# Moving the two-operand work of two stages from GpSimd to VectorE in a two-layer hybrid trunk

## The chip, the cores and the metric

The kernel runs on one core of one Trainium2 chip. The metric is the device time of one execution in microseconds, from the first to the last instruction of the program; three executions of the kernel before gave 3420.28, 3424.99 and 3428.63 us, median 3424.99. Four engines matter here: TensorE (PE in the rows) for products of matrices, VectorE (DVE), ScalarE (ACT) and GpSimd (POOL). SyncE (SP) issues the transfers between DRAM and the on-chip memory SBUF. The matmuls' sums land in PSUM.

## The reference

Two layers run over 1024 latent tokens and 256 context tokens, with 1024 channels. Every layer has an input projection whose columns go to three groups of heads, their joint output projection, and a feed-forward part with a gated convolution. The last layer needs no result for the context.

```
h = rms_norm(x, norm1) * (1 + scale) + shift
c_q, c_kv, k_rope, u, q_s, k_s, v_s = split(h @ w_in)
ya = latent_attention(c_q, c_kv, k_rope)      # 6 heads, all keys; q and k normed, with rotary angles
yb = s5_bidirectional(u)                      # 16 groups of 16 channels, 64 complex states, 2 directions
yc = windowed_attention(q_s, k_s, v_s)        # 6 heads over 2 key heads, a window of 128, sinks
x = x + gate * (concat(ya, yb, yc) @ w_out)
x = x + gate2 * conv_ffn(rms_norm(x, norm2) * (1 + scale2) + shift2)

s5:  a_bar = exp(lam * dt);  b_bar = (a_bar - 1) / lam * b
     h[t] = a_bar * h[t-1] + b_bar u[t];  y[t] = Re(c h[t]) + d u[t];  then a gelu and a gate
rms_norm(x, g) = x * rsqrt(mean(x * x) + eps) * g
```

## The kernel before, in words

All large products are made of three matmuls over a high and a low part of each operand (`ah`, `al`, `wh`, `wl`). The program is one sequence of stages per layer. A list scheduler orders the instructions of each engine by priority and by readiness, so neighbouring pieces of the program are interleaved on each engine; an engine then executes its own list strictly in order.

- **Input projection** (0 to 275 us in layer 0, 1850 to 2085 us in layer 1). For pairs of token tiles (128 tokens each), `s1_pair` makes the windowed keys, `s3` keys and values of the latent attention, `s5q` its queries, `s7` the windowed queries. Each squares its product on ScalarE, sums on VectorE (`ssq`), takes a reciprocal root (`rinv`, by `rsqrt`: two integer steps and three Newton steps, eleven VectorE instructions), multiplies by it (`mulr`), rotates by the angle tables (`rope`, on GpSimd) and stores to DRAM (`kd`, `vd`, `qd`, `sqd`).
- **U projection** (275 to 309 us, 2085 to 2120 us): the S5 channels `u`, in six tiles of the program's tile `f`, stored to `ud`. Loads of the first head's keys (`kn`), queries (`qn`) and values follow on the same SP queue.
- **Latent attention** (309 to 724 us, 2120 to 2492 us): 132 and 120 steps over heads and chunks of queries. It makes scores twice: once for the row maxima (`b<-kh,qh`, read by VectorE as `mx`), and once for the exponentials (`s`), and then the sums over values (`av`). A generator `s5()` runs as `side` between these steps, to a share of its own steps, so that it is done after 5/6 of them (`S5N` holds the number of its steps).
- **S5** works by quarters of the 16 groups. `tables(k)` makes output and input maps (`cv`, `q`) as products of powers with the matrices, `phases(k)` makes rotations `E` for 160 windows by doubling (48 instructions of growing width), both on GpSimd. `maps`, `inputs`, `outputs` are mainly transposes and matmuls on TensorE; `recur` multiplies by `E` on VectorE (`t`, `z`, then a scan over `sv`, then `u`, `Sg`). Ahead of them stand some 150 small VectorE instructions which make the parameters (`s`, `pw`) of the layer from `a_re`, `a_im` and `log_dt`; their transposes on TensorE read `pst`.
- **Modulation vectors** of later stages (`macc<-mw,srow,macc`) run on VectorE beside the attention of layer 0.
- Windowed attention, output projection and feed-forward follow (to 1850 us, and 2492 to 3426 us in layer 1).

The helpers record most operations on one line each in the kernel before: matmuls L65, transposes L74, ScalarE L77, `tt` (two tensors) L80, `ts` (scalars) L93 and L95, `stt` L98. In the order of the kernel after, all VectorE instructions stand at L50, and `tt` on GpSimd at L95.

Of the kernel before, what the change touches and what calls it, by code (L numbers as in the profile page):

```python
# [32 lines left out]
def trunk(ctx, tc, x, c, ctxt, c_ctx, w_mod, b_mod, norm1, w_in, q_lora_g, w_uq, kv_lora_g, w_ukv,  # L33
# [4 lines left out]
    V, S, G, PE = nc.vector, nc.scalar, nc.gpsimd, nc.tensor  # L38
# [19 lines left out]
    mhalf = const.tile([128, 4], F32, name="mhalf")  # L58
# [45 lines left out]
    def load_split(hi, lo, raw, srcs, scale=None):  # L104
        """DRAM pieces into raw, then hi = the rounded value and lo = what is left of it."""
# [9 lines left out]
    class Wsets:  # L115
        """Rotating sets of (rounded, rest, raw) weight tiles over the pools that are open."""
# [49 lines left out]

    def k8(t):
# [73 lines left out]
    def mod_cols(psf, pl, acc, l, nm, k0, n, nj):  # L241
        """Sums over the partitions of acc, n blocks of 128 columns for each of nj."""
# [13 lines left out]
    def mod_gen(l, nm, nj, pl, psf, w):  # L256
        """One modulation vector, with the sums over the rows on the vector engine."""
# [15 lines left out]
    def norm_stats(big, sm, psf, xs, ci, rn, o=0, n=None, eng=None):  # L273
        """rn[p, i] = 1 / rms of token i * 128 + p of the chunk (or of n of its tokens from o)."""
# [3 lines left out]
        for k in range(8):  # L278
# [18 lines left out]
    def norm_apply(tb, rbt, psf, rn, xs, at, A, sh, ci, o=0, n=None, eng=G):  # L297
# [217 lines left out]
    for l in range(2):  # L515
# [63 lines left out]
        def rope(xv, tab, g, t, nh, half, eng=None):  # L579
# [4 lines left out]
            if t >= NL:  # L584
                mul(xv, xv, g.unsqueeze(1).to_broadcast(sh), eng)
                return
# [1490 lines left out]
```

## Time and profile before

| | |
|---|---|
| time of the runs | 3420.28, 3424.99, 3428.63 us |
| span of the profiled execution | 3426.8 us; no other work around the span is in its time |
| TensorE busy | 3253.7 us, 95% |
| VectorE busy | 2339.9 us, 68% |
| ScalarE busy | 1167.5 us, 34% |
| GpSimd busy | 486.9 us, 14%, 787 instructions |

The shares are means over the whole span. How the stages differ is read from windows in time; a recorded VectorE or GpSimd instruction counts as busy from its start to its end, also when it is held up between.

### The profile page before, as it was taken

How to read it: one execution, taken by the hardware profiler on the slowest of the kernel's cores; microseconds unless marked ns; L12 is line 12 of the kernel's file. 1: busy time of each engine (PE TensorE's matmuls, PEld its weight loads, DVE VectorE, ACT ScalarE, POOL GpSimd, SP SyncE). 2: the span in 40 equal slices, each digit the busy share in tenths (PEclk: the TensorE clock that was granted, in tenths of full speed). 3: DMA queues.
4: the chain of work that ended last, by engine and by line, in shares of the span. 5: the costliest groups of instructions: out<-in, count | busy, mean ns of one | idle time of the engine just before them, and what ended most of it. 6: DMA issues, size and time to landing. Idle time of an engine off the chain costs nothing. (4 is left out here: it accounts for less than half of the span.)

```text
span 3426.8 us, 43150 instructions
## 1 busy us (share of the span) xinstructions
PE 3253.7 (95%) x15950; PEld 2597.1 (76%) x15950; DVE 2339.9 (68%) x4391; ACT 1167.5 (34%) x2076; POOL 486.9 (14%) x787
## 2 busy tenths in 40 slices
PE   8999769999999999999999999679999999999999
PEld 5897446667888888888888887446677788888888
DVE  7778786885687766667666768776762665555655
ACT  3532225555152222222223442234563422222221
POOL 2332561000020000000000432471000100000000
PEclk9999789999999999999999999789999999999999
DMA  7434111333512222222212344010324111111211
GB/s 247 132 87 125 32 50 41 98 116 100 166 47 77 64 73 73 64 65 78 62 59 68 101 117 116 18 31 23 87 71 124 44 44 49 56 43 43 62 37 56
DMA packets 401325, 260.84 MB, mean 76 GB/s; under 512 B 173647, under 2 KB 370393, under 8 KB 401113
## 3 DMA queue, kind: packets, MB, share of 16 engines
q1 hardware_dynamic: 400466, 257.80, 26.0%
q8 instruction: 126, 2.06, 0.2%
q14 instruction: 86, 0.70, 0.1%
q10 hardware_dynamic: 647, 0.26, 0.0%
HBM read 206.22 MB, written 49.46 MB: 75 GB/s over the span
## 5 line engine op out<-in xcount | busy, mean ns | idle before, releaser
L65 PE MATMUL u<-ah,wh 128*128 128x512 f32 (+1 forms) x1760 | 649.9, 370 | 2.3 <-ACT ah L77 1.6
L65 PE MATMUL u<-al,wh 128*128 128x512 f32 (+1 forms) x1760 | 648.9, 369 | 1.4 <-POOL al L80 1.1
L65 PE MATMUL u<-ah,wl 128*128 128x512 f32 (+1 forms) x1760 | 648.3, 368 | 0.0
L77 ACT ACTIVATE wh<-raw 128x1024 fp32r<-128x1024 f32 (+3 forms) x184 | 189.2, 1038 | 720.5 <-PE d L65 292.2
L98 DVE SCALAR_TENSOR_TENSOR cv<-u,par,cv 128x511 f32<-128x511 f32 (+2 forms) x616 | 326.1, 555 | 135.6 <-ACT cv L77 130.4
L65 PEld LDWEIGHTS u<-al,wh 128*128 128x128 f32 x1760 | 332.3, 189 | 58.2 <-POOL al L80 2.2
L65 PEld LDWEIGHTS u<-ah,wh 128*128 128x128 f32 x1760 | 332.0, 189 | 57.8 <-ACT ah L77 1.8
L65 PEld LDWEIGHTS u<-ah,wl 128*128 128x128 f32 x1760 | 332.2, 189 | 55.3
L80 DVE TENSOR_TENSOR wl<-raw,wh 128x1024 fp32r<-128x1024 f32 (+3 forms) x184 | 220.1, 1200 | 160.0 <-ACT wh L77 158.9
L98 DVE SCALAR_TENSOR_TENSOR x<-d,g,x 128x512 f32<-128x512 f32 (+2 forms) x307 | 209.5, 685 | 108.8 <-PE d L65 108.6
L98 DVE SCALAR_TENSOR_TENSOR macc<-mw,srow,macc 128x256 f32<-128x256 f32 (+1 forms) x364 | 231.3, 660 | 67.1 <-DMA mw<-in_w_mod_dram 65.8
L77 ACT ACTIVATE cv<-u,par,par 128x512 f32<-128x512 f32 (+1 forms) x220 | 159.7, 728 | 323.1 <-PE u L65 320.9
L65 PE MATMUL av<-p,v 128*65 128x512 f32 (+1 forms) x504 | 260.7, 601 | 0.0
L77 ACT ACTIVATE p<-s 128x512 f32<-128x512 f32 (+1 forms) x252 | 147.6, 586 | 236.4 <-PE s L65 233.1
L65 PE MATMUL d<-ah,wh 128*128 128x512 f32 (+2 forms) x614 | 224.8, 366 | 1.8 <-DVE x L98 1.6
L65 PE MATMUL d<-al,wh 128*128 128x512 f32 (+2 forms) x614 | 223.5, 364 | 0.0
L65 PE MATMUL d<-ah,wl 128*128 128x512 f32 (+2 forms) x614 | 223.4, 364 | 0.0
L1336 DVE TENSOR_REDUCE mx<-b 128x1 f32<-128x512 f32 (+1 forms) x300 | 165.6, 586 | 47.6 <-PE b L65 46.3
L65 PE MATMUL b<-kh,qh 96*128 96x512 f32 (+1 forms) x300 | 124.7, 462 | 63.0 <-DVE ql L98 46.0
L65 PE MATMUL s<-qh,kh 97*128 97x512 f32 (+1 forms) x252 | 154.0, 611 | 0.0
L65 PEld LDWEIGHTS b<-kh,qh 96*128 96x128 f32 x300 | 57.9, 199 | 114.5 <-DVE ql L98 50.8
L65 PE MATMUL av<-sp,sv 128*65 128x384 f32 x320 | 129.0, 492 | 6.5 <-ACT sden L77 3.4
(373 smaller groups left out, 6689.4 us busy)
## 6 DMA issues: line engine op xcount, KB each, us to landing
raw<-in_w_up_dram SPq DMA_DIRECT2D x88, 512.0 KB
mw<-in_w_mod_dram SPq DMA_DIRECT2D x224, 128.0 KB
raw<-in_w_down_dram SPq DMA_DIRECT2D x44, 512.0 KB
mw<-in_w_mod_dram SPq DMA_DIRECT2D x48, 256.0 KB
wm<-in_w_mod_dram SPq DMA_DIRECT2D x16, 512.0 KB
xd<-x SPq DMA_DIRECT2D x32, 256.0 KB
raw<-in_w_in_dram SPq DMA_DIRECT2D x14, 512.0 KB
sqd<-sqb SPq DMA_DIRECT2D x36, 192.0 KB
```

The costliest lines, as they stand in the source:

```text
L65: PE.matmul(out, lhsT, rhs, start=start, stop=stop)
L77: S.activation(out, in_, func, **kw)
L80: (eng or V).tensor_tensor(out, a, b, op=op)
L98: V.scalar_tensor_tensor(out, a, s, b, op0=op0, op1=op1)
L1336: V.tensor_reduce(mx[:, j, i:i + 1], ps[:, :w], axis=AX.X, op=ALU.max)
```

## The change

Everything with two tensor operands on GpSimd in the input projection, the norms and S5 is given to VectorE, apart from the roots. A reciprocal root is now one instruction on GpSimd, the power of -1/2 (`rsqrt_pool`, as the norms had it before). The multiplication by it, with its stores, is put off by one pair of token tiles (`scaling`). The parameters of S5 are made for both layers at once, 2 x 16 columns wide, beside the U projection of layer 0, and go through DRAM (`pmd`, read as `pm`); layer 1 makes none. They hold two power tables `EP` and `EQ`, of which `phases` is one complex product instead of the doubling. Six copies per quarter-independent table, `nct`, `cpx` and `cpl` go from VectorE to ScalarE. S5 yields more often, and its steps are weighed by the VectorE work that they issued (`Metered`, `Weighed`).

```
@@ helpers
+    class Metered:
+            def call(out, *args, **kw):
+                self.load += 100 + max(int(np.prod(a.shape[1:])) for a in (out, *args[:1]) if hasattr(a, "shape"))
+                return fn(out, *args, **kw)
+    V = Metered(nc.vector)
-    mhalf = const.tile([128, 4], F32, name="mhalf")
+    mhalf = const.tile([128, 12], F32, name="mhalf")
-    S5N = [161, 138]
+    S5N = [175700, 166800]
+    class Weighed(Side):
+        def to(self, k):
+            while self.k < k and not self.done:
+                at = V.load
...
+                self.k += 200 + V.load - at
-    def rsqrt(pl, dst, v, shape, tag):
-        i = pl.tile(shape, I32, tag=tag + "i", name="rsi")
-        w = pl.tile(shape, F32, tag=tag + "w", name="rsw")
-        ts(i, v.bitcast(I32), 1, op0=ALU.logical_shift_right)
-        ts(dst.bitcast(I32), i, -1, 0x5F3759DF)
-        for _ in range(3):
-            stt(w, v, -0.5, dst, ALU.mult, ALU.mult)
-            mul(w, w, dst)
-            stt(dst, w, 1.5, dst, ALU.add, ALU.mult)
@@ input projection
-                add(ss[z], ss[z], sq, (eng or (G if k < 6 else V)) if z else V)
+                add(ss[z], ss[z], sq)
-            if k % 2 and eng is G:
-                act(t, t, AF.Identity, bias=sh[:, k, j:j + 1])
-                sub(lo, t, f32(hi), G)
-            else:
-                stt(lo, t, sh[:, k, j:j + 1], f32(hi), ALU.add, ALU.subtract)
+            stt(lo, t, sh[:, k, j:j + 1], f32(hi), ALU.add, ALU.subtract)
-            mul(t1, xv, tb[:, :, :, 0:w].to_broadcast(sh), eng)
+            mul(t1, xv, tb[:, :, :, 0:w].to_broadcast(sh))
...
-            add(xv, t1, t2, eng)
+            add(xv, t1, t2)
-            r = kp.tile([128, 2 * nh], F32, tag="rinv", name="rinv", bufs=2)
-            rsqrt(kp, r, ssq, [128, 2 * nh], f"hn{nh}")
+            r = kp.tile([128, 2 * nh], F32, tag="rinv", name="rinv", bufs=3)
+            rsqrt_pool(r, ssq, 2 * nh)
+        def scaling(fn):
+            if waiting:
+                waiting.pop()()
+            if fn:
+                waiting.append(fn)
...
-            rope(qb, tab_sq, gain["sgq"], t0, 6, 32)
             ssq = ssq_of(sq, 6, 64)
             ts(ssq, ssq, 1.0 / 64, EPS)
-            mulr(qb, qb, rinv(ssq, 6), 6, 64)
-            for i in range(2):
-                for z in range(2):
-                    nc.sync.dma_start(out=sqd[:, t0 + i, :, z, :].rearrange("h p d -> p h d"), in_=qb[:, i])
+            rr = rinv(ssq, 6)
+            rope(qb, tab_sq, gain["sgq"], t0, 6, 32)
+
+            def scaled():
+                mulr(qb, qb, rr, 6, 64)
+                for i in range(2):
+                    for z in range(2):
+                        nc.sync.dma_start(out=sqd[:, t0 + i, :, z, :].rearrange("h p d -> p h d"), in_=qb[:, i])
+            scaling(scaled)
@@ S5
-                mul(t1, pr, cr, G)
-                mul(t2, pi, ci_, G)
-                sub(cv[0], t1, t2, G)
+                mul(t1, pr, cr)
+                yield
+                mul(t2, pi, ci_)
+                yield
+                sub(cv[0], t1, t2)
+                yield
...
-                V.tensor_copy(cpx, unc[:, :, cs])
-                V.tensor_copy(cpl, un[:, :, cs])
+                act(cpx, unc[:, :, cs])
+                act(cpl, un[:, :, cs])
...
-                while n < 160:
-                    m = min(n, 160 - n)
-                    s2 = [128, GQ, m]
-                    er, ei2 = (z[lev][:, gs].unsqueeze(2).to_broadcast(s2) for z in (ec, ei))
-                    cmul(E[0][:, :, n:n + m], E[1][:, :, n:n + m], E[0][:, :, 0:m], E[1][:, :, 0:m], er, ei2, s2,
-                         "pm", G)
+                a = [z[:, :, gs].rearrange("p t g -> p g t").unsqueeze(3).to_broadcast(sh) for z in EP]
+                b = [z[:, :, gs].rearrange("p t g -> p g t").unsqueeze(2).to_broadcast(sh) for z in EQ]
+                Ev = [z.rearrange("p g (a b) -> p g a b", a=10) for z in E]
+                yield from cmul(Ev[0], Ev[1], a[0], a[1], b[0], b[1], sh, "pm")
@@ U projection
+        if l == 0:
+            prm_pool, close_prm = open_pool("prm", side=sd)
+            prms = Side(s5_params(prm_pool, lambda: cps.tile([128, 512], F32, tag="b", name="b", bufs=3)), 30)
+            prms.to(1)
...
-                if f * 3 + ci == 2:
-                    side.to(6)
+                if l == 0:
+                    prms.share(f * 3 + ci + 1, 6)
```

On GpSimd, at the first quarter of S5 in layer 0, the order before holds the tables (`pm`, `cm` are products, `cv`, `q` the maps) and then the doubling of `E`, 60 instructions for a quarter; the first of them are:

```order
L80 TENSOR_TENSOR pm_3830<-pc_3808,ct_3780 128x640
L80 TENSOR_TENSOR pm_3831<-pc_3809,ct_3781 128x640
L80 TENSOR_TENSOR pm_3832<-pc_3808,nct 128x640
L80 TENSOR_TENSOR cv_3826<-pm_3830,pm_3831 128x640
L80 TENSOR_TENSOR pm_3833<-pc_3809,ct_3780 128x640
L80 TENSOR_TENSOR cm_3840<-pq_3810,bb_3776 128x512
L80 TENSOR_TENSOR cv_3827<-pm_3832,pm_3833 128x640
```

After, between the last roots of the input projection and the windowed attention, GpSimd's order has memsets alone; its first rows there are:

```order
L95 TENSOR_TENSOR rinv<-ssq,mhalf 128x12 x2
L95 TENSOR_TENSOR kvr<-kvv,mhalf 128x2
L95 TENSOR_TENSOR rinv<-ssq,mhalf 128x12 x11
L1376 MEMSET v_0_2819 128x10
L1376 MEMSET v_1_2823 128x10
L1256 MEMSET Sg_4092 64x4
```

On VectorE, where `recur` of the first quarter meets the attention's row maxima, the order before is:

```order
L1336 TENSOR_REDUCE mx<-b 128x1 x2
L80 TENSOR_TENSOR strip<-strip,b 16x4x16
L1340 TENSOR_REDUCE nm<-mx 128x4
L80 TENSOR_TENSOR t_4345<-E_4065,sv_4296 128x640
L80 TENSOR_TENSOR t_4348<-E_4066,sv_4296 128x640
L80 TENSOR_TENSOR t_4346<-E_4066,sv_4297 128x640
L80 TENSOR_TENSOR t_4347<-E_4065,sv_4297 128x640
```

After, the phases of the quarter stand ahead of it on the same engine, cut up by the attention's own work:

```order
L50 TENSOR_TENSOR cm_3944<-pm 128x640
L50 SCALAR_TENSOR_TENSOR kl<-b,gcol,kh_2825 96x256
L50 TENSOR_TENSOR cm_3945<-pm 128x640
L50 TENSOR_TENSOR cm_3946<-pm 128x640
L50 TENSOR_TENSOR strip<-strip,b 16x4x16
L50 TENSOR_TENSOR E_3942<-cm_3944,cm_3945 128x640
L50 SCALAR_TENSOR_TENSOR macc<-mw,srow,macc 128x512 x2
L50 TENSOR_TENSOR cm_3947<-pm 128x640
L50 SCALAR_TENSOR_TENSOR ql<-b,gcol,qh 96x512
L50 TENSOR_REDUCE mx<-b 128x1 x6
```

The twelve products of a quarter's tables and the six of its phases have so moved from the first list into this one.

On TensorE, in the U projection of layer 0, the transposes of `kn` stand before its last tiles (`f`) in the order before:

```order
L65 MATMUL f<-ah,wl 128x256
L74 MATMUL b<-ident,kn 96x128 x5
L65 MATMUL f<-ah,wh 128x512
L65 MATMUL f<-al,wh 128x512
L65 MATMUL f<-ah,wl 128x512
L65 MATMUL f<-ah,wh 128x512
L74 MATMUL b<-ident,kn 96x128 x5
```

After, they stand one tile of `f` later, behind the first transpose of `pst`:

```order
L80 MATMUL f<-ah,wl 128x512
L89 MATMUL b<-ident,pst_0_2858 128x16
L89 MATMUL b<-ident,kn 96x128 x4
L89 MATMUL b<-ident,pst_1_2861 128x16
L89 MATMUL b<-ident,pst_2_2864 128x16
L89 MATMUL b<-ident,kn 96x128 x4
L80 MATMUL f<-ah,wh 128x512
```

The transposes of `pst`, which came some 45 rows behind the first `kn` before, are now mixed with them.

## Rows read from the trace of the kernel before

**Rows 1.** The page: engines' totals, and two lines of the 40 slices.
```profile
PE 3253.7 (95%) x15950; PEld 2597.1 (76%) x15950; DVE 2339.9 (68%) x4391; ACT 1167.5 (34%) x2076; POOL 486.9 (14%) x787
...
POOL 2332561000020000000000432471000100000000
PEclk9999789999999999999999999789999999999999
```

**Rows 2.** Windows by stage: each engine's busy us (instructions), granted clock, DMA share, GB/s.
```profile
309.00:330.00 21.00, 21.00 (x86) 12.91 (x85) 20.99 (x151) 9.74 (x19) 0.00 (x0) 1.00 0.68 166
330.00:510.00 180.00, 124.36 (x536) 76.89 (x534) 147.57 (x174) 52.32 (x108) 113.61 (x204) 0.78 0.15 38
510.00:640.00 130.00, 127.58 (x619) 82.17 (x619) 99.25 (x190) 65.52 (x135) 16.64 (x60) 1.00 0.22 60
640.00:724.00 84.00, 82.28 (x366) 53.07 (x365) 70.12 (x153) 44.08 (x89) 0.00 (x0) 1.00 0.41 115
...
2140.00:2320.00 180.00, 128.15 (x541) 79.45 (x540) 131.53 (x157) 55.07 (x110) 105.61 (x204) 0.79 0.10 24
```

**Rows 3.** TensorE in order of time, two attentions: start, us, instruction, idle before and releaser.
```profile
380.74 1.09 PE L74 MATMUL b<-ident,q 128*128 128x128 f32 x4 [18.05 <-DVE mx L1336]
...
2184.09 1.39 PE L65 MATMUL b<-kh,qh 96*128 96x256 f32 x2 [16.95 <-DVE ql L98]
```

**Rows 4.** Ten-microsecond windows: first and last of eighteen in layer 0, last in layer 1.
```profile
330.00:340.00 10.00, 6.58 (x26) 3.66 (x24) 9.85 (x19) 4.31 (x8) 8.08 (x5) 0.93 0.10 27
...
500.00:510.00 10.00, 6.71 (x16) 4.03 (x16) 7.93 (x12) 1.19 (x2) 2.65 (x3) 0.54 0.09 26
...
2310.00:2320.00 10.00, 10.00 (x39) 6.22 (x38) 0.54 (x3) 3.84 (x8) 0.00 (x0) 0.76 0.14 26
```

**Rows 5.** GpSimd in order of time: two rows out of the run without a gap.
```profile
359.08 0.87 POOL L80 TENSOR_TENSOR E<-cm,cm 128x128 f32<-128x128 f32 x2
...
378.18 1.26 POOL L80 TENSOR_TENSOR q<-cm,cm 128x512 f32<-128x512 f32 x1
```

**Rows 6.** VectorE in order of time, the same form twice.
```profile
360.76 19.23 DVE L98 SCALAR_TENSOR_TENSOR macc<-mw,srow,macc 128x512 f32<-128x512 f32 x1
...
388.35 0.74 DVE L98 SCALAR_TENSOR_TENSOR macc<-mw,srow,macc 128x512 f32<-128x512 f32 x1
```

**Rows 7.** VectorE's groups by shape, 290 to 660 us: count, busy us, mean ns, idle before.
```profile
L98 DVE SCALAR_TENSOR_TENSOR macc<-mw,srow,macc 128x512 f32<-128x512 f32 x42 | 73.9, 1782 | 0.9 <-DMA mw<-in_w_mod_dram 0.9
...
L80 DVE TENSOR_TENSOR t<-E,sv 128x640 f32<-128x640 f32 x16 | 21.3, 1350 | 11.0 <-ACT sv L77 11.0
...
L80 DVE TENSOR_TENSOR u<-E,sv 128x640 f32<-128x640 f32 x16 | 12.5, 814 | 0.1
```

**Rows 8.** GpSimd's groups by shape, whole program.
```profile
L80 POOL TENSOR_TENSOR pm<-pc,ct 128x640 f32<-128x640 f32 x24 | 32.1, 1351 | 51.9 <-DVE pc L1017 51.9
```

**Rows 9.** Window of the input projection, layer 0 (columns as in rows 2).
```profile
50.00:300.00 250.00, 237.54 (x1380) 217.68 (x1379) 181.77 (x446) 106.55 (x270) 92.64 (x106) 0.96 0.46 127
```

**Rows 10.** VectorE's groups by shape, 50 to 290 us: the product in the root.
```profile
L80 DVE TENSOR_TENSOR rsw<-rsw,rinv 128x12 f32<-128x12 f32 x45 | 15.9, 352 | 1.4
```

**Rows 11.** GpSimd's groups by shape, whole program: the powers.
```profile
L80 POOL TENSOR_TENSOR rn<-nv,mhalf 128x4 f32<-128x4 f32 x8 | 11.5, 1435 | 35.6 <-DVE nv L95 29.1 <-DMA xd<-x 6.5
...
L80 POOL TENSOR_TENSOR rn<-nv,mhalf 128x2 f32<-128x2 f32 x3 | 2.1, 707 | 4.4 <-DVE rsw L80 3.7 <-DVE nv L95 0.7
```

**Rows 12.** GpSimd and VectorE in order of time, around the first power.
```profile
26.17 1.19 POOL L80 TENSOR_TENSOR rn<-nv,mhalf 128x4 f32<-128x4 f32 x1 [25.73 <-DVE nv L95]
...
26.59 0.74 DVE L98 SCALAR_TENSOR_TENSOR x<-wm,srow,x 128x512 f32<-128x512 f32 x1
```

**Rows 13.** SP's queue in order of time, end of the input projection of layer 0.
```profile
267.81 17.18 SPq L746 DMA_DIRECT2D sqd<-sqb  x12
285.05 1.75 SPq L1305 DMA_DIRECT2D kn<-kd  x2
```

More of the change, by code (lines that the diff above doesn't have):

```diff
@@ L467, in vec2 @@
         return v.rearrange("l (k p) -> (l k) p", p=128)
-    run(prep_x(0, V))
+    run(prep_x(0))
     use_wm(0)
@@ L513, in trunk, with prm_views @@
     applied = ()
+    NPRM = 2 * 144 + 16 + 32 + 2 * 160 + 2 * 256
+    pmd = [dram.tile([128, NPRM], F32, name=f"pmd{l}") for l in range(2)]
+    def prm_views(t):
+        o, r = 0, []
+        for shape in ((9, 16), (9, 16), (16,), (16,), (16,), (10, 16), (10, 16), (16, 16), (16, 16)):
+            n = int(np.prod(shape))
+            v = t[..., o:o + n]
+            if len(shape) == 2:
+                v = (v.rearrange("p (n g) -> p n g", g=16) if len(t.shape) == 2 else
+                     v.rearrange("p l (n g) -> p l n g", g=16))
+            r.append(v)
+            o += n
+        return r[0:2], r[2], r[3:5], r[5:7], r[7:9]
@@ L723, in s5q @@
                         act(sv[:, i, 3 * z:3 * z + 3, :], pv, AF.Square)
-                rope(qb[:, :, :, 64:96], tab_q, gain["gq"][:, :, 64:96], t0, 6, 16)
                 ssq = ssq_of(sq, 6, 96)
@@ L727, in s5q, with scaled @@
                 stt(s3v, s3v, 1.0 / 96, v[:, i0:i0 + 2].unsqueeze(2).to_broadcast([128, 2, 6]))
-                mulr(qb, qb, rinv(ssq, 6), 6, 96)
-                for i in range(2):
-                    nc.sync.dma_start(out=qd[:, t0 + i].rearrange("h p d -> p h d"), in_=qb[:, i])
+                rr = rinv(ssq, 6)
+                rope(qb[:, :, :, 64:96], tab_q, gain["gq"][:, :, 64:96], t0, 6, 16)
+                def scaled(qb=qb, rr=rr, t0=t0):
+                    mulr(qb, qb, rr, 6, 96)
+                    for i in range(2):
+                        nc.sync.dma_start(out=qd[:, t0 + i].rearrange("h p d -> p h d"), in_=qb[:, i])
+                scaling(scaled)
         def s7(t0):
@@ L961, in s5, with cmul @@
[L961 to L973 removed]
+            def cmul(orr, oi, ar, ai, br, bi, shape, tag):
+                t1, t2, t3, t4 = (sp.tile(shape, F32, tag=f"{tag}{i}", name=f"cm{i}") for i in range(4))
+                mul(t1, ar, br)
+                mul(t2, ai, bi)
+                yield
+                sub(orr, t1, t2)
+                mul(t3, ar, bi)
+                yield
+                mul(t4, ai, br)
+                add(oi, t3, t4)
+                yield
@@ L974, in s5 @@
+            pm = sp.tile([128, NPRM], F32, name="pm")
+            nc.sync.dma_start(out=pm, in_=pmd[l])
+            pw, rho, (fr, fi), EP, EQ = prm_views(pm)
             yield
@@ L1060, in tables @@
                 q = [sp.tile([128, GQ, 8, 16], F32, tag=f"q{i}", name=f"q{i}") for i in range(2)]
+                sh = [128, GQ, 8, 16]
+                pr, pi = (pq[i][:, :, gs].rearrange("p t g -> p g t").unsqueeze(3).to_broadcast(sh) for i in range(2))
+                br, bi = (bb[i][:, gs, :].unsqueeze(2).to_broadcast(sh) for i in range(2))
+                yield from cmul(q[0], q[1], pr, pi, br, bi, sh, "pm")
                 sh = [128, GQ, 10, 16]
@@ L1208, in back @@
                     yield
-            tables(0)
+            yield from tables(0)
             yield from windows(0)
-            phases(0)
             for k in range(4):
                 yield from maps(k)
-                if k < 3:
-                    tables(k + 1)
                 if k == 2:
@@ L1219, in s5 @@
                 yield from inputs(k)
+                yield from phases(k)
                 yield from recur(k)
                 if k < 3:
-                    phases(k + 1)
+                    yield from tables(k + 1)
                 yield from outputs(k)
```

387 lines of the change are left out of this document (214 added, 173 removed).

## Prediction

> **What bounds the kernel now.** I read the page first. TensorE is busy for 95% of the span [rows 1], so most of the program can only lose time to a slower TensorE; but the line of its granted clock dips at two places, slices 4 and 5 and slices 25 and 26, 340 to 510 us and 2140 to 2310 us, where the page's GpSimd work also peaks. These are the two latent attentions.
>
> The windows by stage come next. From 330 to 510 us TensorE is busy for only 124 of 180 us, at a mean clock of 0.78; from 2140 to 2320 us for 128 of 180 at 0.79. VectorE is busy for 148 and 132 us there and GpSimd for 114 and 106. Once GpSimd has little left to do (510 to 640 us, 16.6 us busy), TensorE runs 127.6 of 130 us at full clock, with VectorE at 99 [rows 2]. The loss is where GpSimd works.
>
> The order in time of TensorE shows the form of it: a few long stops, 18.05 us before 380.74 and 16.95 us before 2184.09, both released by VectorE [rows 3]; four more are longer than 7 us, and with the short ones they sum to about 53 us in layer 0 and 49 us in layer 1. After each stop the clock is 0.50 or little above for some ten to twenty microseconds. If each of the eighteen ten-microsecond windows of a stretch is counted as busy time by its clock (6.58 by 0.93 in the first, 6.71 by 0.54 in the last), layer 0's stretch holds 103 us of work at full speed, and layer 1's, by the same sum, 110 [rows 4]. So about 77 and 70 us are lost, stops and low clock together.
>
> Why VectorE is late: GpSimd computes two-operand products of S5 without a gap from 359.08 to 379.44 [rows 5]. One VectorE instruction, a `macc` that takes two operands from SBUF, begins at 360.76 and takes 19.23 us; the same form at 388.35, with GpSimd at rest, takes 0.74 [rows 6]. It ends where GpSimd's run ends. The groups by shape show it as means: `macc` 1782 ns x42, about 45 us above the clean price, `t` 1350 ns where `u`, the same shape beside an idle GpSimd, takes 814 [rows 7]. With the copies and `uT` I count 62 us of VectorE time in layer 0 and about 57 in layer 1 that are waiting, recorded as busy.
>
> Here a page bears on it. The Trainium skill, "SBUF — State Buffer", section "Who interferes with whom", says that a VectorE instruction with two SBUF inputs contends with a GpSimd instruction that reads SBUF, and that whoever comes first holds the shared ports for the whole instruction. The trace agrees on who collides, but not on the length: by that rule the wait would last one GpSimd instruction, about 1.3 us, and the 19.23 us above cover a whole run of them. A sum by one instruction a collision would make the gain some tens of microseconds smaller; mine goes by the recorded length.
>
> **The change, part by part.**
>
> *S5 tables and phases to VectorE.* Per quarter of the groups, 12 products of 128x640 and 6 of 128x512. 128x640 costs 0.814 [rows 7], 128x512 four fifths of that, so 12 x 0.814 + 6 x 0.65 = 13.7 us, less a little overlap of neighbours, about 49 us per layer. GpSimd's 1.35 us for the same shape [rows 8] disappears, and with it the long stops: only powers and memsets stay on GpSimd, none of the powers inside the attention. Copies worth some 7 us go from VectorE to ScalarE, which is busy for 52 of 180 us [rows 2].
>
> Layer 0, 330 to 640 us (310 us): TensorE needs 103 + 127.6 = 231 us. VectorE has 147.6 + 99.3 = 247, less 62 waiting, less 7 copies, plus the part of the tables that falls here, about 42: 220 us. The two are nearly level. VectorE at 95% of the stretch would give TensorE its 231; at 83%, which it has from 640 to 724 us [rows 2], the stretch would be 265 us. I take about 88%, 250 us: 60 us won. Both ends stay in the range.
>
> Layer 1 has no modulation sums left in this place, so VectorE has more room: 132 us busy in 180, of which 57 in the stage are waits. TensorE's 110 us then set the pace; I leave 10 us for stops: 60 us won.
>
> *Input projection: the ropes, tables, sums and key parts to VectorE, the reciprocal roots from eleven small VectorE instructions to one GpSimd power.* From 50 to 300 us TensorE is busy for 237.5 of 250 us, VectorE for 182, GpSimd for 93 [rows 9]. GpSimd's work at VectorE's price (0.814/1.351 of it, rows 7 and 8) is at most 56 us more for VectorE. Against it stand 23 roots of 11 instructions at 0.17 us, 43 us clean, and as recorded 65, since they too wait beside GpSimd: the product in the root takes 352 ns in the mean [rows 10]. So VectorE has about 10 us less. TensorE loses just 12.5 us here; a third of that back is 4 us per layer, 8 in all.
>
> The power: 128x4 takes 1435 ns in the mean and 128x2 takes 707 [rows 11]. Twelve columns, as most of the roots here have, are in no row. Bounds: 1.4 us if the columns cost nothing, 4.3 us at 0.36 a column; nearer to the second, so I take 3.5. The multiplication by the root is put off by one pair of token tiles; TensorE needs 4.5 us or more for a pair (24 to 48 matmuls), so 3.5 us is covered, and if that cover were gone it would cost 13 us per layer. Its two-operand form remains on GpSimd, beside VectorE, and could still hold it. A power ran from 26.17 to 27.36 us, and a VectorE instruction with two SBUF operands, 26.59, took its normal 0.74 under it [rows 12]; so I count nothing. The rule of the Trainium skill named above speaks against leaving the power there; that row doesn't show it.
>
> *The end of the projection.* Putting off the multiplication also puts off its DMAs. SP now issues the last of the windowed queries' stores up to 285.0 and only then asks for the first keys (`kn`) [rows 13]. With a pair put off, eight stores instead of four stand after the last product, at about 0.6 us each: `kn` comes 3 to 5 us later. Behind it the U projection's matmuls cover most; in layer 0 the transposes of `pst`, whose loads now stand behind `kn`, come ahead of `kn`'s transposes on TensorE, and its later matmuls are queued behind both. 5 us in layer 0, 3 in layer 1: +8.
>
> *Joint parameters.* Today each layer makes its own just ahead of the attention: from 309 to 330 us VectorE is full (20.99 of 21, 151 instructions), and TensorE too [rows 2]. Layer 0 will make both: instructions twice as wide at nearly the same price, some 215 with the power tables, under the 34 us of the U projection. +3 us for layer 0, bounds 0 and 10; layer 1's share was hidden, so nothing comes back.
>
> *Weighed steps.* They spread S5's steps by their VectorE load instead of their count; S5 ends at the same attention step in both. Nothing, beyond the even spread that the 88% assumes.
>
> Sum: -60 - 60 - 8 + 8 + 3 = -117 us. The profiled execution's span is 3426.8, 1.8 above the median of the runs; 3426.8 - 117 = 3309.8, on the median's scale 3308.
>
> **The rivals.**
>
> *VectorE becomes the bound of layer 0's attention.* For it: 220 us against TensorE's 231. Against: nothing then holds one instruction for 20 us. At 83%, 265 us, 15 more than I took; and if TensorE's many small waits bring its clock down again as the stops do now, another 15. 3338 us.
>
> *The power takes the full 4.3 us or more, or holds VectorE.* For it: each row of rows 11 doubles with the columns. Its cover is then gone: 13 us per layer, 26 in all, 3334 us. If instead each of 30 twelve-column powers held VectorE for its 3.5 us, that is 105 us in two projections where VectorE has some 70 us of room each, so only a part reaches TensorE: much the same time. That second form is what the Trainium skill's "Who interferes with whom" ("SBUF — State Buffer") would make of the power.
>
> *Everything comes back.* TensorE at full speed in both stretches: 77 + 70 + 15 of the projection's idle time less 5: 3270 us.
>
> *Slower.* A twelve-column power of over 10 us, as a chain on GpSimd: per layer ten pairs of 4.5 us and five of 9 would each wait for it, 10 x 5.5 + 5 x 1 = 60 us a layer at 10 us, which eats the gain; at 12 us 2 x (75 + 15) = 180, so 3308 + 180 = 3488. Against it: 128x4 takes 1.4.
>
> *It doesn't do what it says:* the long VectorE times are not GpSimd's doing. Then VectorE only gets more work, and the time is 3425 or more. Against it: the 19 us end with GpSimd's run.
>
> **How the numbers follow.** The forecast, 3290 to 3325, has 0.52; everything back 0.15; VectorE bound 0.15; the power's price 0.10; slower by the power 0.03; not what it says 0.05, half of it within 0.2%. 0.2%, 7 us, is about what a measurement of this kernel can tell from no change. The range 3268 to 3345 leaves out 0.13. Faster 0.92, same 0.03, slower 0.05.
>
> **What would show it.** In the profile after: no VectorE instruction with two SBUF operands over 2 us in the attentions; no clock dip in slices 4, 5, 25 and 26; no stop of TensorE over 5 us from 330 to 460; VectorE near 90% there. Wrong would be: stops as long as before with GpSimd at rest, TensorE waiting for `rinv` in the projection, or stops behind `kn` and `pst` of more than 10 us.

## The result, and the profile after

The changed kernel takes 3323.53 us (median of 3317.84 to 3328.38, four runs) against 3426.2 us of the kernel before in the same rounds: a ratio of 0.9701, 95% interval 0.9687 to 0.9715. The gain is 103 us, where 117 were forecast. The profiled execution's span is 3326.6 us, 100.2 less than before.

The page of the kernel after, the lines that answer to [rows 1]:

```profile
PE 3234.1 (97%) x15950; PEld 2595.8 (78%) x15950; DVE 2261.2 (68%) x4076; ACT 1175.1 (35%) x2142; POOL 106.3 (3%) x99
...
POOL 0220000000000000000000122000000000000000
PEclk9999799999999999999999999899999999999999
```

GpSimd has nothing but memsets left in the two attentions (1.8 us in each). The dip of the clock at slices 25 and 26 has gone from layer 1's attention but for one slice, and the one at slices 4 and 5 is one slice long. The windows by stage, as [rows 2]; they span the same microseconds as before, though the attention itself now ends at 687 instead of 724:

```profile
309.00:330.00 21.00, 20.99 (x86) 12.28 (x84) 17.76 (x98) 10.24 (x26) 0.00 (x0) 0.97 0.17 32
330.00:510.00 180.00, 157.62 (x695) 101.41 (x694) 159.84 (x293) 78.22 (x181) 0.79 (x8) 0.86 0.23 67
510.00:640.00 130.00, 126.98 (x602) 83.40 (x601) 113.72 (x209) 69.18 (x141) 0.96 (x10) 1.00 0.22 63
```

From 330 to 510 us TensorE is busy for 158 us, where it was for 124; VectorE is busy for 160 of 180 us, 89%, which is about the rate that the prediction took. But the mean clock is 0.86, not 1. VectorE's groups by shape in layer 0's attention, which answer to [rows 7]:

```profile
L50 DVE SCALAR_TENSOR_TENSOR macc<-mw,srow,macc 128x512 f32<-128x512 f32 x56 | 39.7, 742 | 1.7 <-DMA mw<-in_w_mod_dram 1.7
...
L50 DVE TENSOR_TENSOR cm<-pm 128x640 f32<-128x640 f32 x16 | 19.5, 1245 | 0.0
...
L50 DVE TENSOR_TENSOR t<-E,sv 128x640 f32<-128x640 f32 x16 | 12.7, 815 | 0.0
```

`macc` went from 1782 to 742 ns and `t` from 1350 to 815, their clean prices. No VectorE instruction of the attentions, nor of the projections, takes over 2 us. The new `cm<-pm`, the products of the phases, take 1245 ns, not the 815 of their shape.

TensorE in order of time has no stop over 5.4 us left in the projections and attentions, where six of over 7 us stood before ([rows 3] show two of them). These are the four longest of layer 0's attention:

```profile
356.21 1.94 PE L89 MATMUL b<-ident,q 128*128 128x128 f32 x8 [5.36 <-DVE q L50]
361.08 0.58 PE L80 MATMUL b<-cv,bb 64*16 64x128 f32 x2 [2.93 <-DVE cv L50]
...
386.73 0.37 PE L89 MATMUL b<-ident,nm 128*4 128x128 f32 x1 [2.40 <-DVE nm L50]
...
412.56 0.27 PE L89 MATMUL b<-ident,nm 128*4 128x128 f32 x1 [2.45 <-DVE nm L50]
```

All lie between 350 and 413 us. Three windows of that time show what goes with such stops, small as they are: a clock between 0.50 and 0.74, and in two of the three a VectorE without any room.

```profile
350.00:360.00 10.00, 2.78 (x12) 1.84 (x10) 9.37 (x18) 5.95 (x18) 0.00 (x0) 0.74 0.26 67
380.00:390.00 10.00, 4.91 (x13) 2.92 (x13) 10.00 (x18) 0.95 (x2) 0.00 (x0) 0.50 0.06 15
410.00:420.00 10.00, 5.66 (x16) 3.76 (x16) 10.00 (x20) 3.10 (x6) 0.00 (x0) 0.64 0.24 58
```

To compare stages between kernels I measure each from TensorE's order: a projection, with its U projection, from the first `tk` to the first `s`; an attention from the first `s` to the first `av<-sp` of the windowed one. In five-microsecond windows over such a stage, idle is what TensorE is not busy, and the loss by the clock is busy time less busy time by its clock.

| us | projection 0 | attention 0 | its idle | its loss by the clock | projection 1 | attention 1 | its idle | its loss by the clock |
|---|---|---|---|---|---|---|---|---|
| before | 258.6 | 415.3 | 59.8 | 20.0 | 239.9 | 372.4 | 53.6 | 17.5 |
| after | 252.7 | 382.5 | 27.9 | 22.5 | 223.9 | 321.1 | 13.0 | 10.6 |

So the attentions give 32.8 and 51.3 us, the projections 5.9 and 16.0; the rest of the program takes 6 us more. In layer 0's attention the idle time is halved, and the loss by the clock is as large as before. VectorE's busy time in it has not fallen. Here are the whole stage before and after, and then its part up to 430 us and the rest:

```profile
308.70:724.00 415.30, 355.52 (x1605) 225.30 (x1604) 338.23 (x668) 171.72 (x351) 130.40 (x266) 0.91 0.25 67
...
304.10:686.70 382.60, 354.72 (x1597) 229.48 (x1597) 338.11 (x715) 182.58 (x395) 1.76 (x18) 0.92 0.27 74
304.10:430.00 125.90, 106.67 (x404) 67.46 (x404) 108.05 (x292) 48.76 (x114) 0.40 (x4) 0.77 0.22 59
430.00:686.70 256.70, 248.05 (x1195) 162.02 (x1194) 230.06 (x424) 133.81 (x282) 1.36 (x14) 1.00 0.30 82
```

All of the loss by the clock, and 19 of the 28 us idle, lie before 430 us.

A stage's time is read from one profiled execution. Where a run below leaves a stage as it is, layer 0's attention takes 381.1 to 383.8 us and layer 1's 317.9 to 323.4, so I read little from differences smaller than that.

### The profile page after: what moved, and what is told of

It reads as the page before. It is cut to its first block, busy times and chain, and to the rows that moved or that the text cites. A ratio compares the mean times of both kernels' runs of the same rounds, so it can differ in the third digit from the quotient of the medians.

```text
span 3326.6 us, 42024 instructions
## 1 busy us (share of the span) xinstructions
PE 3234.1 (97%) x15950; PEld 2595.8 (78%) x15950; DVE 2261.2 (68%) x4076; ACT 1175.1 (35%) x2142; POOL 106.3 (3%) x99
## 4 chain that ended last, share of the span: by engine, by line
PE 83%; DVE 11%; DMA 2%; ACT 2%; issue 1%; SPq 1%; POOL 0%; ACTq 0%; DVEq 0%; POOLq 0%
PE u L80 32%; PE d L80 11%; PE av L80 6%; PE tk L80 5%; PE o L80 5%; PE dx L80 5%; PE f L80 5%; PE s L80 5%; PE b L80 4%; PE b L89 2%; DVE mx L50 2%; DVE macc L50 1%; DVE cm L50 1%; DVE al L50 1%; DVE Sg L50 1%
## 5 line engine op out<-in xcount | busy, mean ns | idle before, releaser
L50 DVE SCALAR_TENSOR_TENSOR macc<-mw,srow,macc 128x256 f32<-128x256 f32 (+1 forms) x364 | 186.9, 539 | 64.0 <-DMA mw<-in_w_mod_dram 62.4
L50 DVE SCALAR_TENSOR_TENSOR x<-dx,g,x 128x512 f32<-128x512 f32 (+2 forms) x141 | 97.3, 690 | 51.4 <-PE dx L80 51.3
```

The lines of the kernel that those rows point to most:

```text
L50: return fn(out, *args, **kw)
```

## The experiments

All ratios are to the kernel before, in the same rounds; the kernel after has 0.9701.

### One part of the change undone

**S5's products back on GpSimd.** The 18 products of a quarter's tables and phases get the engine back:

```
-                yield from cmul(q[0], q[1], pr, pi, br, bi, sh, "pm")
+                yield from cmul(q[0], q[1], pr, pi, br, bi, sh, "pm", G)
...
-                mul(t1, pr, cr)
+                mul(t1, pr, cr, G)
```

> The kernel after, with the 18 two-operand products of a quarter of S5 (tables and phases) back on GpSimd, in the same order and with the same weights of the steps. If a run of two-operand products on GpSimd is what holds VectorE up, the long VectorE instructions come back in both attentions and the time rises by 60 to 100 us, to about 3385 to 3425. If the gain came from the other parts (joint parameters, copies on ScalarE, weighed steps, roots), it stays within 15 us of 3323.

Measured: 3363.95 us, 0.9831 [0.9807, 0.9856]. 40 us come back, 25.8 in the attention of layer 0 and 12.9 in that of layer 1; the projections stay. It is between the two expectations, short of the first. VectorE in order of time, and GpSimd beside it:

```profile
447.70 8.45 DVE L50 TENSOR_TENSOR t<-E,sv 128x640 f32<-128x640 f32 x1 [2.26 <-POOL pm L95]
```

```profile
449.15 1.56 POOL L95 TENSOR_TENSOR cv<-pm,pm 128x640 f32<-128x640 f32 x1
450.65 4.83 POOL L95 TENSOR_TENSOR cm<-pm 128x640 f32<-128x640 f32 x3
```

The long VectorE instruction is back, and it ends at 456.15, 0.7 us after GpSimd's run does (450.65 + 4.83). There are three such places in the two attentions, none over 9 us: the new phases are 6 products a quarter where the doubling had 48, and the runs are shorter. So the move from GpSimd is worth 39 us of the 84 that the attentions gained; the shorter phases, the joint parameters, the weighed steps and the copies on ScalarE are with the other 45, and no run here parts those.

Nor are the 39 us all due to held instructions. The three take 21.7 us together, and TensorE also waits for GpSimd itself, which makes the tables more slowly (1.35 us a product, [rows 8], where VectorE takes 0.815):

```profile
357.94 1.11 PE L89 MATMUL b<-ident,q 128*128 128x128 f32 x4 [9.05 <-POOL q L95]
...
365.86 0.60 PE L80 MATMUL b<-cv,bb 64*16 64x128 f32 x2 [5.13 <-POOL cv L95]
```

In the kernel after, the same two stops are 5.36 and 2.93 us. How much of the 39 us is the hold and how much the slower engine, the run does not show.

**The projection's products back on GpSimd**, the roots still powers:

```
-            mul(t1, xv, tb[:, :, :, 0:w].to_broadcast(sh))
+            mul(t1, xv, tb[:, :, :, 0:w].to_broadcast(sh), G)
...
-                    add(tot[:, :n], tot[:, :n], sq[:, :n])
+                    add(tot[:, :n], tot[:, :n], sq[:, :n], G)
```

> The kernel after, with the ropes, their tables, the sums of squares and the key parts of the input projection back on GpSimd; the roots stay powers. If VectorE's waits beside GpSimd cost TensorE time in the projection, 8 to 15 us are lost, 3331 to 3338. If the projection's 22 us of gain are those of the roots alone, no change, 3320 to 3327.

Measured: 3358.52 us, 0.982 [0.9796, 0.9844], 35 us lost, over twice the larger expectation. Projection 0 takes 276.2 us, more than before the change, and projection 1 takes 231.1. The mechanism is not the one expected alone: a power now waits in GpSimd's own queue. GpSimd and TensorE in order of time:

```profile
71.77 2.77 POOL L95 TENSOR_TENSOR tab<-tab,sgk 128x256 f32<-128x256 f32 x4 [44.56 <-DVE ssq L50]
74.50 0.73 POOL L95 TENSOR_TENSOR ra<-ks,tab 128x256 f32<-128x256 f32 x1
75.18 1.02 POOL L95 TENSOR_TENSOR rn<-nv,mhalf 128x4 f32<-128x4 f32 x1
```

```profile
76.75 1.22 PE L80 MATMUL sm<-ident,rb 128*128 128x128 f32 x4 [4.28 <-DVE rb L50]
```

The norm's power `rn` stands behind the rope table and a rope, and TensorE waits 4.28 us for what follows it. From 70 to 90 us the clock is 0.66, where the kernel after has 1.00. Roots on GpSimd cost time as long as the ropes are there.

**The roots of the heads and key latents as eleven VectorE instructions again**, the rest as after:

```
-            rsqrt_pool(r, ssq, 2 * nh)
+            rsqrt(kp, r, ssq, [128, 2 * nh], f"hn{nh}")
```

> The kernel after, with the roots of the heads and of the key latents as eleven VectorE instructions again; ropes and S5 stay on VectorE. VectorE gets about 22 us more work in each projection, where it is busy for 140 of 224 us. If it has that room, 0 to 5 us are lost, 3323 to 3328; if the chain of a root is what the projection's matmuls wait for, 10 to 20 us, 3333 to 3343.

Measured: 3321.48 us, 0.9719 [0.9689, 0.9749], no difference. Projection 0 takes 252.9 us, projection 1 takes 220.1. VectorE is busy for 191 instead of 157 us in projection 0 and has room for it. The powers are worth nothing by themselves. The projection's gain lies in the rest: the ropes, tables and sums on VectorE and the put-off multiplication, which no run parts.

### Where layer 0's attention loses

**The modulation sums later**: `mods.share` begins 60 steps later.

```
-                mods.share(done, nsteps + 15)
+                mods.share(max(done - 60, 0), nsteps - 45)
```

> The kernel after, with the modulation sums of layer 0's attention begun 60 of 132 steps later (the same work, in the lighter half). If layer 0 falls short of the forecast because VectorE's work is crowded into the first 130 us of its attention (parameters, then tables), 10 to 20 us are won, 3303 to 3313. If VectorE's volume over the whole attention is the bound, or only the wait for the parameters through DRAM, it changes by less than 5 us or gets slower at the end of the attention.

Measured: 3331.03 us, 0.9738 [0.9714, 0.9763]. Layer 0's attention takes 379.5 us, 3 less than after, and the windowed attention behind it 121.1, 4 more. Idle time (26.1 us) and loss by the clock (20.4) hardly move. VectorE is busy for 328.8 us of the stage instead of 338.1, so 9 us less of its work bring 3. Crowding by these sums is not the main cause. The second expectation holds, but it covers both VectorE's volume and the wait for the parameters, and leaves that open.

**The parameters made earlier**, beside the windowed keys of layer 0's projection (the call of `s5_params` moves, with its pool):

```
...
+        if l == 0:
+            prm_pool, close_prm = open_pool("prm", side=sd)
+            prms = Side(s5_params(prm_pool, sbank), 30)
+            prms.to(1)
         for t in range(4, NT - 2 * l, 2):
             s1_pair(t, part[t - 4:t - 2] if l else None)
+            prms.share(t // 2 - 1, 3)
...
```

> The kernel after, with the joint S5 parameters made during the windowed keys of layer 0's input projection instead of beside the U projection and the attention's first steps. Theory: layer 0 falls short because its parameters run on VectorE until 342 us and come back from DRAM at 349, so that S5's tables come late while TensorE's list already holds their transposes. Then the attention of layer 0 gets 15 to 30 us shorter, the projection up to 10 longer, in all 3300 to 3315. Rival, VectorE's rate through the whole attention is the bound: it gets shorter by less than 10 us, 3318 or more.

Measured: 3313.45 us, 0.9671 [0.9654, 0.9689]. Layer 0's attention takes 354.1 us, 28 less, with 15.3 us idle and 7.1 lost by the clock: near the upper end of what was expected. But the stage has also lost 28 us of VectorE's work, from 338.11 to 309.97:

```profile
322.40:676.50 354.10, 338.78 (x1604) 221.01 (x1603) 309.97 (x559) 182.95 (x396) 1.76 (x18) 0.98 0.29 77
```

So the run does not part earlier tables from a less loaded VectorE. Projection 0 takes 272.7, 20 more, twice what was allowed for. ScalarE in order of time shows why:

```profile
167.74 0.42 ACT L92 ACTIVATE kb<-tk,kvr 128x192 f32<-128x192 f32 x1 [30.14 <-DMA pmd<-prmJ]
```

The pool of the next part lies in the memory of the parameters and waits until they are stored. TensorE's one long stop there is 20.41 us. VectorE makes the parameters until 163.4 us, and ScalarE goes on at 167.74, when they are stored. The 20 us are thus a wait through memory for the end of VectorE's chain, not a lack of room on VectorE.

**Beside the windowed queries instead**, in the memory of the latents, which are no longer needed there:

```
+        if l == 0:
+            scaling(None)
+            close_cp()
+            prm_pool, close_prm = open_pool("prm", side=other(sd))
...
         for t in range(0, ntq, 2):
             s7(t)
+            if l == 0:
+                prms.share(t // 2 + 1, 5)
...
```

> The kernel after, with the joint S5 parameters made beside the windowed queries (the last 42 us of layer 0's projection, where VectorE is busy for 6 to 12 of every 20 us), not beside the windowed keys, which took 20 us for it. If it is the room on VectorE that decides, the projection gets no more than 5 us longer and the attention of layer 0 keeps the 28 us: 3295 to 3303. If the parameters' small instructions delay the projection wherever they stand, its 20 us are lost again: 3310 to 3318.

Measured: 3324.32 us, 0.9703 [0.968, 0.9725]. The time lies above both expectations. Layer 0's attention keeps the 28 us (354.2); projection 0 loses 31 (284.0), as in the second expectation but more, and not for its reason. TensorE and ScalarE again:

```profile
312.83 0.79 PE L80 MATMUL f<-ah,wh 128*128 128x512 f32 x1 [31.01 <-ACT us L92]
```

```profile
312.18 1.36 ACT L92 ACTIVATE us<-f 128x512 f32<-128x512 f32 x3 [43.24 <-DMA pmd<-prmJ]
```

The copy of the U projection's first result has its tile in the parameters' memory. Here all 31 us are one stop.

**S5 begun ten steps later** in both layers, to end at the same step:

```
-                side.share(done, nsteps * 5 // 6)
+                side.share(max(done - 10, 0), nsteps * 5 // 6 - 10)
```

> The kernel after, with S5 in both layers begun ten attention steps later and ended at the same step. If TensorE's stops at 350 to 361 us, where the transposes of late tables stand ahead of the attention's own matmuls, are what the start of the attention loses, layer 0's attention gets 8 to 15 us shorter, 3308 to 3315. If the amount of VectorE work is the bound, crowding it into 100 instead of 110 steps costs 0 to 10 us.

Measured: 3300.53 us, 0.9631 [0.9613, 0.9649]: 23 us faster than the kernel after, more than expected. Layer 0's attention is 8.4 us shorter (374.1), as expected; layer 1's is 14.3 shorter (306.8), which I had not expected, with 8.6 us idle and no loss by the clock at all. The stops at 356 and 361 are gone; the one behind `nm` is 4.45 us long (at 394). Layer 1 makes no parameters, so there it is not they that come late. In the kernel after, all of its loss by the clock (10.6 us) follows one window at the start of S5, in which VectorE is full and no stop of TensorE is over 2 us:

```profile
2090.00:2100.00 10.00, 5.67 (x24) 3.06 (x22) 10.00 (x16) 3.93 (x9) 0.00 (x0) 0.78 0.00 0
2100.00:2110.00 10.00, 9.66 (x30) 5.88 (x31) 6.62 (x10) 5.55 (x20) 0.00 (x0) 0.50 0.00 0
2110.00:2120.00 10.00, 10.00 (x49) 6.91 (x48) 5.64 (x10) 5.07 (x10) 0.00 (x0) 0.53 0.04 8
```

Beginning S5 later takes this away, with VectorE's busy time in the stage unchanged (246 us).

**The small power table with neighbouring elements**, one copy by ScalarE for each part:

```
+            EQc = [sp.tile([128, 16, 16], F32, name=f"EQc{i}") for i in range(2)]
+            for z, w in zip(EQc, EQ):
+                act(z, w.rearrange("p t g -> p g t"))
...
-                b = [z[:, :, gs].rearrange("p t g -> p g t").unsqueeze(2).to_broadcast(sh) for z in EQ]
+                b = [z[:, gs, :].unsqueeze(2).to_broadcast(sh) for z in EQc]
```

> The kernel after, with the small power table of the phases copied once by ScalarE so that VectorE reads it with neighbouring elements instead of every sixteenth. The 32 products take 1.245 us each now; with the price of the other 128x640 products, 0.815, VectorE gets 6.9 us less work per layer. If the stride is the reason, the products fall to 0.82; the time falls by 3 to 8 us if VectorE bounds the attention of layer 0, and by less than 3 if TensorE's stops come from elsewhere.

Measured: 3322.87 us, 0.9701 [0.9686, 0.9716], no difference. The products do what was expected:

```profile
L50 DVE TENSOR_TENSOR cm<-pm,EQc 128x640 f32<-128x640 f32 x16 | 12.6, 816 | 0.0
```

6.9 us of VectorE fewer per layer shorten layer 0's attention by 2.8 (379.7) and layer 1's by 0.9. So VectorE's volume does not set the time one to one, although it is busy for 88% of the stage; that it counts for something, 2.8 us for 6.9, is not excluded.

**All three together**: parameters beside the windowed queries, S5 ten steps later, the table copied.

> Parameters beside the windowed queries, S5 begun ten steps later in both layers, and the small power table copied for neighbouring elements. If the three act on different waits, their gains add: 25 in layer 0 for the parameters, 15 in layer 1 for the later start, 0 to 5 for the table: 3275 to 3290. If the parameters and the later start cure the same wait in layer 0, its attention stays near 354 us, and the sum is 3285 to 3290.

Measured: 3296.99 us, 0.9629 [0.9602, 0.9656], above the range. The attentions are at 341.5 and 303.9 us, with no loss by the clock in either and 10.1 and 6.8 us idle: 41 and 17 us less than after. VectorE's busy time in layer 0's attention is down by 41 us too, to 296.5. The wait for memory ahead of the U projection (29.12 us) takes back most of layer 0's part. It is not measurably better than the later start alone. With twenty steps:

> The same with S5 begun twenty steps later, so that it runs in 90 and 80 steps. If the first tables are what S5 is late with, nothing more is won: within 4 us of the ten steps. If VectorE's rate bounds the rest, crowding costs 5 to 15 us.

Measured: 3316.11 us, 0.9681 [0.9657, 0.9706]. The attentions take 352.2 and 312.5 us: crowding costs 11 and 9 us. The second expectation holds; between ten and twenty steps the amount of work does begin to count.

### GpSimd and VectorE side by side

Loops on dummy tiles behind the end of the kernel, so that the time of the runs themselves tells nothing.

```
+    for g, v in ((gset, vtt), (gtt, vtt), (gtt, vcopy), (gtt, vred), (gset, vtt), (gpow, vtt), (gtt, None)):
...
+        for i in range(24):
+            if g and i % 2 == 0:
+                g()
+            if v:
+                v()
```

> The kernel after, with loops on dummy tiles behind its end: twelve GpSimd instructions without a gap, beside 24 instructions of VectorE, for GpSimd products of 128x640, memsets and powers, and VectorE products, copies and reductions of 128x512 from SBUF. If VectorE is held for a whole run of GpSimd, one VectorE product takes about 15 us, as the 19.23 us before; if it is held one GpSimd instruction at a time, each takes 1.3 to 2 us. Memsets should hold nothing. Powers hold VectorE 2 us or more each, or nothing at all, as the first row of the kernel before has it.

GpSimd in order of time, then VectorE:

```profile
3340.80 23.27 POOL L95 TENSOR_TENSOR mgo<-mga,mgb 128x640 f32<-128x640 f32 x12 [6.73 <-DVE mga L50]
3372.71 20.07 POOL L95 TENSOR_TENSOR mgo<-mga,mgb 128x640 f32<-128x640 f32 x12 [8.64 <-DVE mga L50]
3398.74 8.20 POOL L2149 MEMSET mgo<- 128x640 f32 x12 [5.96 <-DVE mga L50]
```

```profile
3340.68 31.20 DVE L50 TENSOR_TENSOR mo<-ma,mb 128x512 f32<-128x512 f32 x23
...
3372.59 25.09 DVE L50 COPY mo<-ma 128x512 f32<-128x512 f32 x23
...
3398.63 16.54 DVE L50 TENSOR_REDUCE mo<-ma 128x1 f32<-128x512 f32 x23
...
3416.14 16.84 DVE L50 TENSOR_TENSOR mo<-ma,mb 128x512 f32<-128x512 f32 x23
```

VectorE's first two rows outlast GpSimd's, so they hold both kinds of instructions, those beside GpSimd and those after it. Single instructions of either kind:

```profile
3343.34 1.90 DVE L50 TENSOR_TENSOR mo<-ma,mb 128x512 f32<-128x512 f32 x1
...
3366.83 0.69 DVE L50 TENSOR_TENSOR mo<-ma,mb 128x512 f32<-128x512 f32 x1
...
3376.39 1.64 DVE L50 COPY mo<-ma 128x512 f32<-128x512 f32 x1
...
3395.40 0.43 DVE L50 COPY mo<-ma 128x512 f32<-128x512 f32 x1
```

Beside GpSimd's products a VectorE product takes 1.90 us, alone 0.69; a copy, which has one operand, takes 1.64 and 0.43. GpSimd's own products follow each other every 23.27/12 = 1.94 us. The engines take turns, one instruction at a time: the second expectation, not the 15 us. (The 1.36 us that the next expectation quotes is 31.20/23, a mean over both kinds.) Beside memsets, reductions start every 0.72 us. The fourth row runs beside twelve powers (2.49 us each): a product starts every 0.73 us there, as it does alone, so the powers hold next to nothing, as [rows 12] had it.

> The kernel after, with dummy loops behind its end again: twelve GpSimd products of 128x640 into one tile, into two tiles by turns, and with operands repeated by a stride of zero as in S5's tables, beside VectorE products of 128x512. In the first such run the two engines took turns, 1.36 us a VectorE product. If writing one tile again and again made GpSimd let go between its instructions, two tiles by turns hold a VectorE product for several instructions, 4 us or more; if the repeated operands make the difference, only the third kind does; if neither, all take 1.3 to 1.4 us.

```profile
3357.66 15.78 DVE L50 TENSOR_TENSOR mo<-ma,mb 128x512 f32<-128x512 f32 x10
...
3386.79 15.78 DVE L50 TENSOR_TENSOR mo<-ma,mb 128x512 f32<-128x512 f32 x10
...
3416.20 7.17 DVE L50 TENSOR_REDUCE mo<-ma 128x1 f32<-128x512 f32 x10
```

With two tiles by turns and with repeated operands the products take 1.64 us while GpSimd runs (the first of the ten in each row takes 0.69), taking turns again; reductions, one operand, start every 0.72 us beside GpSimd's products and are not held. So neither of the two makes a hold over many instructions. In S5 itself both forms occur. In the run with its products back on GpSimd, VectorE's scans take turns with them (two in 3.63 us, where one alone takes 0.46), and at 447.70 a product waits for the rest of a run:

```profile
398.39 3.63 DVE L50 TENSOR_TENSOR_SCAN sv<-pm,z 128x160 f32<-128x160 f32 x2
```

What lets a run of GpSimd keep a VectorE instruction out for 8 to 20 us, and not in these loops, stays open.

## Why the prediction was right, and where it was not

The direction and the range held; the sum was 14 us too good, with larger errors in both directions under it. The attentions gave 84 us where 120 were taken; the projections with the U projections gave 22 where the terms -8, +8 and +3 make a loss of 3; the rest of the program took 6 more. That these nearly cancel is luck. Of the four signs named, two came (no VectorE instruction over 2 us in the attentions, VectorE near 90%) and two did not: the clock still dips in slices 4 and 25, and one stop of 5.36 us is left.

**GpSimd's runs hold VectorE, and their end frees the attentions: right in the main.** The clean prices came back in the kernel after, and with the products on GpSimd again so did a VectorE instruction of 8.45 us that ends with GpSimd's run. That run gives back 39 of the attentions' 84 us, some of them by waits for GpSimd itself.

**Layer 0's attention, -60: measured -32.8.** This term failed, in two steps. The first is the clock: I took a slower TensorE to be over with the long stops, but the loss by the clock did not go, 22.5 us after 20.0. Stops of 2 to 5 us between 350 and 413 us go with as low a clock there. The second is VectorE's work. Its share came out as taken, 88% of the stage, but its busy time did not fall (338.2 and 338.1 us), where the terms -62, -7 and +49 make 20 us less. S5's products took 59 us, where 49 were counted, and the parameters, priced at +3, did not stay under the U projection: the stage holds 28 us of them, twice the 14 of before.

Two causes meet at the start of S5. One is that its tables come late. VectorE in order of time:

```profile
341.65 0.23 DVE L50 TENSOR_TENSOR prmJ<-pt,pt 128x64 f32<-128x64 f32 x1
349.35 0.76 DVE L50 TENSOR_TENSOR cm<-pm,bn 128x256 f32<-128x256 f32 x2 [7.47 <-DMA pm<-pmd]
```

The parameters last until 342 us instead of ending under the U projection, at 304; they return from DRAM at 349; the tables start only then, while TensorE's list already holds their transposes ahead of the attention's own matmuls. The stops at 356 and 361 are this wait. The other cause is that VectorE, once it has the tables to make, has no room, and the attention's maxima (`mx`, `nm`) stand between S5's products. This is what TensorE's stop of 2.40 us before 386.73 ends with, in a window with VectorE at 10.00 of 10 us:

```profile
385.79 0.81 DVE L50 TENSOR_TENSOR t<-E,sv 128x640 f32<-128x640 f32 x1
386.52 0.15 DVE L50 TENSOR_REDUCE nm<-mx 128x4 f32<-128x12 f32 x1
```

Taking the parameters out of that place gave 28 us, starting S5 later 8, and both with the table 41. But the first and the last also took 28 and 41 us of VectorE's work out of the stage, so they do not part late tables from a loaded VectorE. Against the load alone speak the modulation sums and the copied table, where 9.3 and 6.9 us less of VectorE's work gave 3.0 and 2.8, and the clock of 1.00 from 430 us on with VectorE still at 90%. At that rate the parameters' 28 us would give some 9 to 11 (an estimate from those two runs, each hardly clear of the noise), and the rest would be the wait. What is shown is that the loss lies before 430 us in the main, and that 28 us come back with the parameters gone; how they divide between the two causes is open. So the rival on VectorE's rate is borne out in part: VectorE is without room at the start of S5, not through the whole attention, and it had the fall of the clock with small waits right. The measured time lies midway between the forecast and that rival's 3338.

**Layer 1's attention, -60: measured -51.3.** The same loss in small, at the start of S5 and without any parameters: 14 us come back when S5 starts ten steps later.

**The projections, -8: measured -5.9 and -16.0, with the U projections.** Mis-sized to the other side. From the first `tk` to the first U matmul layer 0 gains 11 us; layer 1 gains 16 up to its attention. I had given back a third of the idle time; in layer 1 it is 10 of 13.4 us. The reason that I gave, VectorE's balance with the shorter roots, is wrong: with the old roots VectorE has more to do and nothing is lost. With the ropes, tables and sums back on GpSimd 35 us are lost.

**The power.** A 128x12 power takes 2.49 us, where 3.5 was taken:

```profile
L95 POOL TENSOR_TENSOR rinv<-ssq,mhalf 128x12 f32<-128x12 f32 x28 | 69.8, 2493 | 170.4 <-DVE ssq L50 170.4
```

The delayed multiplication covers it for TensorE, which waits for no `rinv` in the two projections; VectorE waits 48 us for it there, in time that it has to spare. It holds next to nothing. Both rivals that rest on the power fell. By the Trainium skill, "SBUF — State Buffer", section "Who interferes with whom", a VectorE instruction with two SBUF inputs contends with a GpSimd instruction that reads SBUF; for the powers the trace hardly shows it (a product takes 0.69 to 0.75 us beside them, 0.69 alone), for products of 128x640 it does (1.90 us).

**The end of layer 0's projection, +8 with its parameters: +5.** From the first U matmul to the first `s` it is 38.4 us, where it was 33.3. But not as told: SP asks for `kn` 8.6 us after the first U matmul, where it was 9.6 before. The delay by the put-off stores that I took from [rows 13] is not there.

```profile
255.73 18.49 SPq L953 DMA_DIRECT2D sqd<-sqb  x12
274.28 1.75 SPq L1399 DMA_DIRECT2D kn<-kd  x2
```

In layer 1, where +3 was taken, the same stretch is 4.7 us shorter (34.0 after 38.7).

**The phases' price.** I took 0.814 us for all twelve 128x640 products; four a quarter take 1.245, since one operand is read with a step of sixteen elements. The Trainium skill, "SBUF — State Buffer", has a note under "Door 1: The DMA port swizzle" that each access to another line of 16 bytes costs extra, and the copied table agrees, with 0.816. It cost no time that the runs can tell.

## What to carry to other kernels

Where a stage loses time to a few long stops, price what the stops do to TensorE's clock apart from the stops, and ask which shorter stops are left: here they went with as low a clock. Add up anew what the engine that takes over the work has to do in that stage; its share can come out as forecast while its work does not. Where work is fed into an engine's fixed order between other work, look first at its start: what its first pieces wait for stands ahead of everything else, and starting it a little later can be worth more than making it cheaper. A move of work to an earlier place can be paid for in memory too: in three runs the next pool waited for the last reader of the one before.

## What the hardware showed that was not expected

- Twelve GpSimd products of 128x640 without a gap and a stream of VectorE products on SBUF take turns, one instruction each, in dummy loops of three kinds: a VectorE product of 0.69 us takes 1.64 to 1.90. In the kernel one VectorE instruction waits for a whole run, 19.23 us before and 8.45 us with S5's products back on GpSimd. No run here settles what makes the difference.
- A VectorE copy with one operand is held beside GpSimd's products (1.64 us against 0.43 alone), a reduction is not (0.69 both ways). In the kernel before, one copy (`cpx`) was held for 20.31 us.
- A power of 128x12 on GpSimd takes 2.49 us in the kernel after, of 128x4 some 1.26 to 1.44 in the mean. Beside a stream of VectorE products the 128x12 power took 2.27 to 2.72 us, alone 2.27; the products took at most 0.75 us instead of 0.69.
- In layer 1's attention one window of ten microseconds with 4.3 us idle, and no stop over 2 us, is followed by twenty at a clock of 0.50 and 0.53: the idle time costs 4 us and the clock 11.
